# Reordering the opening of the first FFN and splitting the last row tile of a two-layer encoder step on one NeuronCore

## The chip, the core and the metric

The kernel runs on one NeuronCore of a Trainium2 chip. The five engines that matter here have queues of their own: TensorE (PE in the profile, with its weight loads as PEld), VectorE (DVE), ScalarE (ACT), GpSimd (POOL) and SyncE (SP, which only issues DMAs here). The metric is the device time of one execution in microseconds; the figure quoted is the median of several runs. A profile shows one further execution, and its span runs from the first to the last instruction of the program.

## The reference

Two layers are computed over 640 tokens of width 1024: 512 prompt tokens and 8 running streams of 16 tokens. Each layer is

```python
xp = xp + 0.5 * _swiglu(_rmsnorm(xp, norm_ffn1[l]), w_ffn1_gu[l], w_ffn1_down[l])
mp, ... = _mixer(_rmsnorm(xp, norm_mix[l]), ...)     # convolution branch and attention branch
xp = xp + mp
xp = xp + 0.5 * _swiglu(_rmsnorm(xp, norm_ffn2[l]), w_ffn2_gu[l], w_ffn2_down[l])
...
y_prompt = _rmsnorm(xp, norm_final)
```

with `_swiglu(h) = (silu(h @ w_g) * (h @ w_u)) @ w_down`, an inner width of 2816, and an RMS norm that divides a token by the root of the mean of its squares and multiplies by a gain. The same is done to the sample tokens. Everything is fp32.

## The kernel before

**Products in three passes.** The activations live in SBUF as eight tiles `x[0..7]`, 128 features by 640 tokens. Each fp32 operand is split into a high part, rounded to fp32r by ScalarE (`whi` for weights, `xhi` for activations), and a low part, the difference, made by VectorE (`wlo`, `xlo`). A product is the sum of three matmuls: high by high, and the two mixed ones. Thus no weight slab can be used before ScalarE has made its `whi` (L369) and VectorE its `wlo` (L375). A slab is 128x1024; `prep` (L355) makes `whi` and puts the `wlo` on a list, `flush` (L373) issues the list, `source` and `ahead` (L304, L397) make the sums of raw weights that some slabs need, and `slab(True)` (L380) takes the next slab and calls `prep` two slabs ahead without the flush.

**Seven products in place of eight.** Most groups multiply 2 by 2 blocks in a scheme with seven block products, in the order X11, X21, XN6, XT5, XT7, X22, XT4. One block product is 12 matmuls of 320 columns. The sums that such a scheme needs, of inputs, of weights and of outputs, are VectorE's work for the most part.

**The opening** (`opening`, L755) is the first FFN's start. Nine dummy matmuls run while the first loads arrive. Then, for each k of 0 to 7, `Expand.plain(k)` (L656) splits x[k] times its gain, L774 and L775 split 256 columns of a weight slab, and after each odd k the four products of two k's go into the PSUM accumulators `first[0]` and `first[1]`. After that come the squares of x[0..7] on ScalarE (`square`), added up on VectorE (`add`, tile `ssuma`). After the squares of k = 4 and k = 5, `out(0)` and `out(1)` copy the two accumulators out of PSUM (L795, L803). There are two accumulators of that kind, so the next product, `ps[2]`, waits for `out(0)`. In the middle of `ps[2]` TensorE sums `ssuma` over the partitions (`npsa`), ScalarE takes the root (L742), VectorE the reciprocal, and `spread` makes `rhoa`, the factor of every token, by which all later outputs of the FFN are multiplied.

**The first down unit** (`down_rows`, L1159). In the first FFN the inner tiles 0 to 3 are made by `opening`, and 4 and on by `gate_up` (L895). Between tiles 5 and 6 stands the first unit of the down projection, for output rows 0 to 3 (`second` is false) of inner tiles 0 to 3 (`sent` is true). Its block products go through PSUM pairs `daa`, `dba`, `dca`; `take` (L1199) adds a pair into x on VectorE, `stage` copies one out on ScalarE, and `send` adds it into x by DMA. `tail` (L1181) runs what tile 5 left over: silu(g) times rho (L1032), the product with u (L1069), and the split of the result (L1076, L1124). `place("d1")` then runs three combining instructions of that pair (L1134, L1136). The block XT4 of this unit writes the pair `daa` that `take(a, 1, t2)` has read.

**The end** (`Final.all`, L2168). The last down projection and the final norm are done in two shapes. Tokens 0 to 255 stay in feature order (`product`, `take`, `out`). The other 384 tokens are turned: three row tiles i = 0, 1, 2 of 128 tokens, each in two PSUM banks `rows[i][0]` and `rows[i][1]` of 512 features. For each, `half(i, h)` does six matmuls, `square(i, h)` is a sum of squares on ScalarE, `part` and `inverse` make the factor, `ahead` multiplies by the gain on VectorE before the factor is known, `scaled` multiplies by gain and factor in one VectorE instruction, and `rest` multiplies what `ahead` made by the factor on ScalarE.

**What sets the order.** In the opening, in the first down unit and at the end the mode is `order(ORDERED)`: TensorE, VectorE and ScalarE each take their instructions in the program's order. From inner tile 6 of an FFN up to its last chunk only TensorE's order is fixed (L1304), and the scheduler places the others.

All semaphores are set by the framework in which the kernel is written.

Of the kernel before, what the change touches and what calls it, by code (L numbers as in the profile page):

```python
# [16 lines left out]
P = 128  # L17
HP = P // 2
D = 1024
# [176 lines left out]
def trunk(ctx: ExitStack, tc: tile.TileContext, xin, wst, small, pbias, samplebias, kcache, vcache, gfin,  # L196
# [387 lines left out]
    class Expand(Stats):  # L584
# [71 lines left out]
        def plain(self, m):  # L656

            kp, odd = divmod(m, 2)
            n = f"{self.name}_{kp}"
            g = sm[:, self.goff + m : self.goff + m + 1]  # L660

            def low(lo, src, hi):
                DVE.scalar_tensor_tensor(out=lo, in0=src, scalar=g, in1=hi.bitcast(F32),
                                         op0=ALU.mult, op1=ALU.subtract)

            if odd:
                hi, lo = (z[:, 3:5] for z in self.ops[kp])
                ACT.activation(hi, halves(x[m]), AF.Copy, scale=g)
                low(lo, halves(x[m]), hi)
                return tuple(tuple(z[:, a] for a in range(2)) for z in (hi, lo))  # L670
            hi, lo = (self.fp.tile([P, 7, HT], F32R, name=f"x{i}{n}", tag=f"x{i}{kp}") for i in ("hi", "lo"))
            self.ops.append((hi, lo))
            if kp % 2 == 0:
                self.side = [hp.tile([P, T], F32R, tag=f"h{i}", name=f"x2{i}{n}") for i in ("hi", "lo")]
            c = slice(kp % 2 * HT, (kp % 2 + 1) * HT)
            out = (hi[:, X11], self.side[0][:, c]), (lo[:, X11], self.side[1][:, c])
            for a, (h, l) in enumerate(zip(*out)):
                src = x[m][:, a * HT : (a + 1) * HT]
                ACT.activation(h, src, AF.Copy, scale=g)
                low(l, src, h)  # L680
            return out
# [73 lines left out]
    def opening(fp, name, goff, n, pairs, tails):  # L755

        ACT.copy(early, epst)
        ex = Expand(fp, name, goff)  # L760
        h = []
        for i in range(2):
            ready.append(tuple(wp.tile([P, CH], F32R, tag=f"w{t}", name=f"w{t}{i}", bufs=3) for t in ("hi", "lo")))

        idle, row = att("idle"), tmp("row")[:, :P]
        DVE.memset(row, 1.0)
        for i in range(WAKE):
            PE.matmul(idle[:, :P], ones.to_broadcast([P, P]), row, start=i == 0, stop=i == WAKE - 1)
        first = [acc(f"po{name}_{i}") for i in range(2)]
        for k in range(KT):  # L770
            h.append(ex.plain(k))
            c = slice(k // 2 * 2 * P, (k // 2 + 1) * 2 * P)
            raw, (whi, wlo) = raws[k % 2], ready[k % 2]
            ACT.copy(whi[:, c], raw[:, c])  # L774
            DVE.tensor_tensor(out=wlo[:, c], in0=raw[:, c], in1=whi[:, c].bitcast(F32), op=ALU.subtract)  # L775
            if k % 2:
                for p, w in zip(first, ready):
                    for kk in (k - 1, k):
                        multiply(p, [z[:, kk * P : (kk + 1) * P] for z in w], h[kk], kk == 0, kk == KT - 1)
        used[0] = 2  # L780

        mixed = [z for kp in range(NP) for z in [ex.mixed(kp)] * 2]
        made = {2: (0,), 3: (1, 2, 3), 4: (4,), 5: (5, 6), 6: (7,)}
        us, gs, ps = [], [], first

        def out(i):

            j, up = divmod(i, 2)
            if not up:
                gs.append(tmp(f"g{name}_{j}"))  # L790
                if j:
                    scaled(gs[j], ps[i], ex.rho)
                    ACT.activation(gs[j], gs[j], AF.Silu)
                else:
                    ACT.copy(halves(gs[j]), two(ps[i]))  # L795
                return
            u = tmp(f"u{name}_{j}") if j > 1 else fp.tile([P, T], F32, tag="cap", name=f"u{name}_{j}", bufs=6)
            us.append(u)
            if j:
                scaled(u, ps[i], ex.rho)  # L800
                DVE.tensor_tensor(out=u, in0=u, in1=gs[j], op=ALU.mult)
            else:
                ACT.copy(halves(u), two(ps[i]))  # L803

        def begun():
            ex.total(att(f"nps{name}"))
            ex.root()
            ex.diagonal()

        at = {2: {6: begun}, 3: {1: lambda: ex.spread([att(f"nbc{name}_{a}")[:, :HT] for a in range(2)])}}  # L810
        prep(2)
        flush()
        for k in range(KT):
            ex.square(k)
            ex.add()
            if k in (4, 5):
                out(k - 4)
        for i in range(2, 2 * n):
            ps.append(acc(f"po{name}_{i}"))
            product(ps[i], h, at.get(i, {}))  # L820
            if i > 2:
                out(i - 1)
            if i == 3:
                g, u = gs[0], us[0]
                DVE.tensor_tensor(out=g, in0=g, in1=ex.rho, op=ALU.mult)
                ACT.activation(g, g, AF.Silu)
                DVE.tensor_tensor(out=u, in0=u, in1=ex.rho, op=ALU.mult)
            flush()
            for m in made.get(i, ()):
                next(mixed[m])  # L830
            if i == 3:
# [12 lines left out]
        ahead()  # L844
        out(2 * n - 1)
        tails += [lambda: pairs[1].odd(us[3]), pairs[1].mixed, pairs[1].fourth]
        ex.rest = None
        return ex
# [310 lines left out]
    def down_rows(fp, n, ms, pairs, tails, later, sent):  # L1159
# [49 lines left out]
        behind.clear()  # L1209
        prep(used[0] + 1)  # L1210
        begin()
        if not second:
            tail()
        flush()
        place("d1")
        mul(b, s0, 1, X21, True)
        with soon():
            take(b, 0, t1)
# [11 lines left out]
        with soon():  # L1230
            take(a, 1, t2, -0.5)
        send(c5, 1, t2)
        flush()
        ahead()
        mul(c, s2, 1, X22, False)
# [923 lines left out]
    class Final:  # L2159


        def __init__(self):
            self.st = Stats("f")
            self.ssum = pool[0].tile([P, FEAT], F32, tag="ssum", name="fsum", bufs=1)
            self.acc = sp.tile([P, 2 * GROUPS], F32, tag="facc", name="facc", bufs=1)
            self.root = sp.tile([P, 3 * GROUPS], F32, tag="froot", name="froot", bufs=1)

        def all(self, ops):  # L2168
# [37 lines left out]
            for k in range(1, 4):  # L2206
                self.out(k, rr)
            self.half(1, 0, ops, ws)
            self.square(1, 0)
            self.part(1)  # L2210
            self.half(1, 1, ops, ws)
# [1 line left out]
            for k in range(4, KT):  # L2213
                self.out(k, rr)
            self.inverse(1)
            for h in range(2):
                self.scaled(1, h)
            self.half(2, 0, ops, ws)
            self.square(2, 0)
            self.ahead(2)  # L2220
            self.part(2)
            self.half(2, 1, ops, ws)
            self.square(2, 1)
            self.ahead(2, 1)
            self.inverse(2)
            self.last(2)

        def product(self, m, ops, ws):
# [19 lines left out]
                PE.matmul(self.rows[i][h][:, o * P : (o + 1) * P], x[m][:, c], ident, is_transpose=True,  # L2248
                          start=o == 0, stop=False, skip_group_check=True)

        def half(self, i, h, ops, ws):

            tokens = slice(FEAT + i * P, FEAT + (i + 1) * P)
            c = slice(h * D // 2, (h + 1) * D // 2)
            for k, ((xh, xl), (wh, wl)) in enumerate(zip(ops, ws)):
                for j, (z, w) in enumerate(((xh, wh), (xl, wh), (xh, wl))):
                    PE.matmul(self.rows[i][h], z[:, tokens], w[:, c], start=False,
                              stop=k == len(ops) - 1 and j == 2, skip_group_check=True)

        def column(self, i, o):  # L2260
            return self.root[:, 3 * i + o :][:, 0:1]

        def square(self, i, h):
            ACT.activation(tmp(f"sqr{i}{h}")[:, : D // 2], self.rows[i][h], AF.Square,
                           accum_out=self.acc[:, 2 * i + h :][:, 0:1])

        def part(self, i):
            DVE.tensor_scalar(out=self.column(i, 0), in0=self.acc[:, 2 * i :][:, 0:1], scalar1=1.0 / D,
                              scalar2=EPS, op0=ALU.mult, op1=ALU.add)

        def inverse(self, i):
            ACT.activation(self.column(i, 1), self.acc[:, 2 * i + 1 :][:, 0:1], AF.Sqrt,
                           bias=self.column(i, 0), scale=1.0 / D)
            DVE.reciprocal(self.column(i, 2), self.column(i, 1))

        def ahead(self, i, h=0):
            c = slice(h * D // 2, (h + 1) * D // 2)
            DVE.tensor_tensor(out=self.y[i][:, c], in0=self.rows[i][h], in1=self.g[:, c], op=ALU.mult)

        def last(self, i):  # L2280
            for o, w, engine in ((0, 3, DVE), (3, 2, ACT), (5, 3, DVE)):
# [198 lines left out]
```

## Time and profile before

| | |
|---|---|
| time, median of 3 runs | 2467.57 us (2467.53 to 2467.99) |
| time of the profiled execution | 2468.21 us |
| its span | 2466.4 us |
| PE busy | 2458.3 us (100%) |
| DVE busy | 2196.8 us (89%) |
| ACT busy | 1396.9 us (57%) |
| POOL busy | 329.7 us (13%) |
| HBM over the span | 101 GB/s |
| granted TensorE clock | 1.000 |

A row of a timeline gives start and length in us, the engine, the source line, the operation, the output and inputs by their names in the program, the shape, and in brackets how long the engine sat idle before it and what ended that. "xN" means that N such instructions were merged into one row, and the length is then that of the whole group. A row of a view of waits gives the engine and line that waited, what released it, the total in us, the number of waits and the longest. An "engine" with a q at its end is the engine's queue, which issues DMAs.

### The profile page before, as it was taken

How to read it: one execution, taken by the hardware profiler on the slowest of the kernel's cores; microseconds unless marked ns; L12 is line 12 of the kernel's file. 1: busy time of each engine (PE TensorE's matmuls, PEld its weight loads, DVE VectorE, ACT ScalarE, POOL GpSimd, SP SyncE). 2: the span in 40 equal slices, each digit the busy share in tenths (PEclk: the TensorE clock that was granted, in tenths of full speed). 3: DMA queues.
4: the chain of work that ended last, by engine and by line, in shares of the span. 5: the costliest groups of instructions: out<-in, count | busy, mean ns of one | idle time of the engine just before them, and what ended most of it. 6: DMA issues, size and time to landing. Idle time of an engine off the chain costs nothing.

```text
span 2466.4 us, 44136 instructions
## 1 busy us (share of the span) xinstructions
PE 2458.3 (100%) x17234; PEld 2409.1 (98%) x17234; DVE 2196.8 (89%) x3725; ACT 1396.9 (57%) x2246; POOL 329.7 (13%) x495
## 2 busy tenths in 40 slices
PE   9999999999999999999999999999999999999999
PEld 9999999889999999999999999998899999999998
DVE  7999999888998899998799999988889979999997
ACT  6555556665655555555665555566656556555555
POOL 0211112211110001011001111121110000111111
PEclk9999999999999999999999999999999999999999
DMA  4553444335443334445334343453454433444444
GB/s 156 138 126 100 121 118 122 111 112 175 116 130 123 87 102 112 108 118 123 107 97 109 109 119 101 118 129 102 139 160 122 122 115 94 108 113 107 113 118 118
DMA packets 115282, 290.93 MB, mean 118 GB/s; under 512 B 13216, under 2 KB 53664, under 8 KB 115072
## 3 DMA queue, kind: packets, MB, share of 16 engines
q1 hardware_dynamic: 69840, 220.10, 28.3%
q0 software_dynamic: 44800, 67.75, 14.6%
q8 instruction: 135, 2.21, 0.4%
q14 instruction: 75, 0.61, 0.1%
q10 hardware_dynamic: 432, 0.25, 0.0%
HBM read 241.57 MB, written 7.94 MB: 101 GB/s over the span
## 4 chain that ended last, share of the span: by engine, by line
PE 97%; DMA 1%; DVE 1%; ACT 0%; issue 0%; SPq 0%; DVEq 0%; ACTq 0%
PE pab L469 13%; PE paa L469 11%; PE pcb L469 6%; PE pca L469 6%; PE daa L1175 6%; PE dab L1175 5%; PE po L445 5%; PE qa L469 4%; PE pbb L469 3%; PE pba L469 3%; PE dca L1175 3%; PE dcb L1175 3%; PE ma_qk L469 2%; PE ma_cv L469 2%; PE pv L1872 2%; PE qc L469 2%
## 5 line engine op out<-in xcount | busy, mean ns | idle before, releaser
L369 ACT CAST whi<-raw 128x1024 fp32r<-128x1024 f32 (+1 forms) x564 | 500.1, 892 | 376.1 <-DVE raw L298 63.6
L375 DVE TENSOR_TENSOR wlo<-raw,whi 128x1024 fp32r<-128x1024 f32 (+1 forms) x602 | 580.0, 967 | 135.4 <-ACT whi L369 131.8
L369 ACT CAST whi<-s 128x1024 fp32r<-128x1024 f32 (+1 forms) x166 | 155.2, 935 | 287.3 <-issue 111.3
L469 PE MATMUL pab<-xhib,whi 128*128 128x320 f32 x704 | 217.5, 309 | 0.0
L469 PE MATMUL pab<-xhib,wlo 128*128 128x320 f32 x704 | 217.0, 308 | 0.0
L469 PE MATMUL pab<-xlob,whi 128*128 128x320 f32 x704 | 217.0, 308 | 0.0
L469 PE MATMUL paa<-xhia,whi 128*128 128x320 f32 x640 | 197.7, 309 | 0.0
L469 PE MATMUL paa<-xloa,whi 128*128 128x320 f32 x640 | 197.5, 309 | 0.0
L469 PE MATMUL paa<-xhia,wlo 128*128 128x320 f32 x640 | 197.4, 308 | 0.0
L375 DVE TENSOR_TENSOR wlo<-s,whi 128x1024 fp32r<-128x1024 f32 (+1 forms) x169 | 179.1, 1060 | 3.6 <-ACT whi L369 3.6
L1197 POOL DMA_DIRECT2D x<-c_a x80 | 70.0, 1014 | 568.3 <-ACT ahia L1076 244.8
L1197 POOL DMA_DIRECT2D x<-c_b x72 | 63.1, 1009 | 582.2 <-ACT ahib L1076 205.8
L469 PEld LDWEIGHTS pab<-xhib,whi 128*128 128x128 f32 x704 | 132.1, 188 | 0.9 <-issue 0.9
L469 PEld LDWEIGHTS pab<-xlob,whi 128*128 128x128 f32 x704 | 132.2, 188 | 0.0
L469 PEld LDWEIGHTS pab<-xhib,wlo 128*128 128x128 f32 x704 | 132.1, 188 | 0.0
L469 PEld LDWEIGHTS paa<-xhia,whi 128*128 128x128 f32 x640 | 120.1, 188 | 0.6 <-issue 0.4
L469 PEld LDWEIGHTS paa<-xloa,whi 128*128 128x128 f32 x640 | 120.2, 188 | 0.2 <-DVE xloa L712 0.2
L469 PEld LDWEIGHTS paa<-xhia,wlo 128*128 128x128 f32 x640 | 120.1, 188 | 0.0
L298 DVE TENSOR_TENSOR raw<-s,raw 128x512 f32<-128x512 f32 x166 | 113.1, 682 | 0.0
L469 PE MATMUL pcb<-xhib,wlo 128*128 128x320 f32 x352 | 108.7, 309 | 0.0
L469 PE MATMUL pcb<-xlob,whi 128*128 128x320 f32 x352 | 108.5, 308 | 0.0
L469 PE MATMUL pcb<-xhib,whi 128*128 128x320 f32 x352 | 108.5, 308 | 0.0
(896 smaller groups left out, 8248.3 us busy)
## 6 DMA issues: line engine op xcount, KB each, us to landing
raw<-in_wst SPq DMA_DIRECT2D x374, 512.0 KB, 3.7
x<-c_a POOLq DMA_DIRECT2D x80, 160.0 KB, 4.4
x<-c_b POOLq DMA_DIRECT2D x72, 160.0 KB, 3.5
one<-in_wst POOLq DMA_DIRECT2D x40, 256.0 KB, 3.5
lent<-in_wst POOLq DMA_DIRECT2D x36, 256.0 KB, 3.8
kc<-in_kcache SPq DMA_DIRECT2D x32, 256.0 KB, 5.0
vc<-in_vcache SPq DMA_DIRECT2D x16, 512.0 KB, 4.6
x<-u_a POOLq DMA_DIRECT2D x40, 160.0 KB, 4.3
```

The lines of the kernel that those rows point to most:

```text
L298: DVE.tensor_tensor(out=out, in0=a, in1=b, op=op)
L369: ACT.copy(hi[:, d], src[:, c])
L375: DVE.tensor_tensor(out=lo, in0=src, in1=hi.bitcast(F32), op=ALU.subtract)
L445: PE.matmul(ps[:, a, :HT], w, x[a] if isinstance(x, tuple) else x[:, a * HT : (a + 1) * HT], start=first and j == 0 and not seeded, stop=l ...
L469: PE.matmul(ps, a, b, start=start and kp == 0 and j == 0, stop=stop and kp == NP - 1 and j == 2, skip_group_check=True)
L1175: PE.matmul(ps[u], w, y, start=start and i == 0 and j == 0, stop=i == 1 and j == 2, skip_group_check=True)
L1197: POOL.dma_start(x[ms[2 * u + r]][:, cols], z[:, u], accum_op=ALU.add)
L1872: PE.matmul(pv[t], xx[:, t * P : (t + 1) * P], w[:, kk * AW : (kk + 1) * AW], start=c == 0 and kk == 0 and j == 0, stop=c == KT // 2 - 1 a ...
```

## The change

Five edits in the first FFN and the end:

1. The odd tile x[1] is split in two column halves, ScalarE's cast and VectorE's difference in turn (`plain`).
2. The high part of the very first weight piece (k = 0) is made by VectorE, ahead of all else, in place of ScalarE.
3. `out(0)` and `out(1)` stand after the squares of k = 2 and 3 in place of 4 and 5.
4. In the first down unit `tail()` and `place("d1")` are put off until `take(a, 1, t2)` and its `send`.
5. At the end: row tile 1 gets `ahead(1)` between its first half and its squares, and then only its second half is scaled by VectorE; `rest(1)` scales the first on ScalarE, which issues its DMA too. The last half of row tile 2 is done in two quarters of 256 columns of the same bank, each with its matmuls, squares and product with the gain; the sum of squares gets one more column, and a second `part` adds the first quarter's.

```diff
@@ plain
             if odd:
                 hi, lo = (z[:, 3:5] for z in self.ops[kp])
-                ACT.activation(hi, halves(x[m]), AF.Copy, scale=g)
-                low(lo, halves(x[m]), hi)
+                for c in (slice(0, 1), slice(1, 2)) if m == 1 else (slice(0, 2),):
+                    ACT.activation(hi[:, c], halves(x[m])[:, c], AF.Copy, scale=g)
+                    low(lo[:, c], halves(x[m])[:, c], hi[:, c])
@@ opening
         first = [acc(f"po{name}_{i}") for i in range(2)]
+        c = slice(0, 2 * P)
+        DVE.tensor_copy(ready[0][0][:, c], raws[0][:, c])
         for k in range(KT):
...
-            ACT.copy(whi[:, c], raw[:, c])
+            if k:
+                ACT.copy(whi[:, c], raw[:, c])
...
             ex.square(k)
             ex.add()
-            if k in (4, 5):
-                out(k - 4)
+            if k in (2, 3):
+                out(k - 2)
@@ down_rows
         begin()
-        if not second:
+        put_off = sent and not second
+        if not second and not put_off:
             tail()
         flush()
-        place("d1")
+        if not put_off:
+            place("d1")
         mul(b, s0, 1, X21, True)
...
         send(c5, 1, t2)
+        if put_off:
+            tail()
+            place("d1")
         flush()
         ahead()
@@ Final
-            self.acc = sp.tile([P, 2 * GROUPS], F32, tag="facc", name="facc", bufs=1)
+            self.acc = sp.tile([P, 2 * GROUPS + 1], F32, tag="facc", name="facc", bufs=1)
...
             self.half(1, 0, ops, ws)
+            self.ahead(1)
             self.square(1, 0)
             self.part(1)
             self.half(1, 1, ops, ws)
...
             self.inverse(1)
-            for h in range(2):
-                self.scaled(1, h)
+            self.scaled(1, 1)
+            self.rest(1)
             self.half(2, 0, ops, ws)
             self.square(2, 0)
             self.ahead(2)
             self.part(2)
-            self.half(2, 1, ops, ws)
-            self.square(2, 1)
-            self.ahead(2, 1)
-            self.inverse(2)
+            for e in range(2):
+                self.half(2, 1, ops, ws, e)
+                self.square(2, 1, e)
+                self.ahead(2, 1, e)
+                if e == 0:
+                    self.part(2, 1)
+            self.inverse(2, 2)
             self.last(2)
...
+        def piece(e):
+            return slice(0, D // 2) if e is None else slice(e * D // 4, (e + 1) * D // 4)
...
+        def part(self, i, h=0):
+            z = self.column(i, 0)
+            if h:
+                DVE.scalar_tensor_tensor(out=z, in0=self.acc[:, 2 * i + h :][:, 0:1], scalar=1.0 / D, in1=z,
+                                         op0=ALU.mult, op1=ALU.add)
...
```

`half`, `square` and `ahead` get an argument e that cuts their columns with `piece`; `inverse` gets the column of the sum of squares that it takes.

More of the change, by code (lines that the diff above doesn't have):

```diff
@@ L2249, in turned, with half @@
                           start=o == 0, stop=False, skip_group_check=True)
-        def half(self, i, h, ops, ws):
+        @staticmethod
+        def piece(e):
+            return slice(0, D // 2) if e is None else slice(e * D // 4, (e + 1) * D // 4)
+        def half(self, i, h, ops, ws, e=None):
             tokens = slice(FEAT + i * P, FEAT + (i + 1) * P)
-            c = slice(h * D // 2, (h + 1) * D // 2)
+            o = self.piece(e)
+            c = slice(h * D // 2 + o.start, h * D // 2 + o.stop)
             for k, ((xh, xl), (wh, wl)) in enumerate(zip(ops, ws)):
                 for j, (z, w) in enumerate(((xh, wh), (xl, wh), (xh, wl))):
-                    PE.matmul(self.rows[i][h], z[:, tokens], w[:, c], start=False,
+                    PE.matmul(self.rows[i][h][:, o], z[:, tokens], w[:, c], start=False,
                               stop=k == len(ops) - 1 and j == 2, skip_group_check=True)
@@ L2261, in column, with square, inverse, ahead @@
             return self.root[:, 3 * i + o :][:, 0:1]
[L2263 to L2272, printed above, removed]
+        def square(self, i, h, e=None):
+            o = self.piece(e)
+            ACT.activation(tmp(f"sqr{i}{h}{e}")[:, o], self.rows[i][h][:, o], AF.Square,
+                           accum_out=self.acc[:, 2 * i + h + (e or 0) :][:, 0:1])
+        def part(self, i, h=0):
[3 more added lines that the diff above has]
+                                         op0=ALU.mult, op1=ALU.add)
+            else:
+                DVE.tensor_scalar(out=z, in0=self.acc[:, 2 * i :][:, 0:1], scalar1=1.0 / D,
+                                  scalar2=EPS, op0=ALU.mult, op1=ALU.add)
+        def inverse(self, i, h=1):
+            ACT.activation(self.column(i, 1), self.acc[:, 2 * i + h :][:, 0:1], AF.Sqrt,
                            bias=self.column(i, 0), scale=1.0 / D)
             DVE.reciprocal(self.column(i, 2), self.column(i, 1))
-        def ahead(self, i, h=0):
-            c = slice(h * D // 2, (h + 1) * D // 2)
-            DVE.tensor_tensor(out=self.y[i][:, c], in0=self.rows[i][h], in1=self.g[:, c], op=ALU.mult)
+        def ahead(self, i, h=0, e=None):
+            o = self.piece(e)
+            c = slice(h * D // 2 + o.start, h * D // 2 + o.stop)
+            DVE.tensor_tensor(out=self.y[i][:, c], in0=self.rows[i][h][:, o], in1=self.g[:, c], op=ALU.mult)
         def last(self, i):
```

## The prediction

> **What bounds the kernel now.** The page's first part and the chain of work that ended last are read first, then who waited for whom on PE in the first 300 us.
>
> ```profile
> PE 2458.3 (100%) x17234; PEld 2409.1 (98%) x17234; DVE 2196.8 (89%) x3725; ACT 1396.9 (57%) x2246; POOL 329.7 (13%) x495
> PE 97%; DMA 1%; DVE 1%; ACT 0%; issue 0%; SPq 0%; DVEq 0%; ACTq 0%
> PE poa L445 <- ACT ga L795: 0.7, 1, 0.7
> PE poa L445 <- ACT whi L774: 0.3, 1, 0.3
> PE poa L445 <- DVE xloa L663: 0.3, 1, 0.3
> PEld daa L1175 <- DVE x L1202: 0.4, 1, 0.4
> ```
>
> PE is the path for 97% of the span. The change removes no matmul: it can gain only where PE stands still, which is 0.7 + 0.3 + 0.3 us in the opening, 0.4 us in the first down unit, and what runs behind the last matmul. Against that, VectorE is busy for 89% and for longer stretches without a gap, so I ask at each edit what VectorE finishes next.
>
> **The opening (edits 1 to 3).** Rows of PE's chain, of ScalarE and VectorE, and VectorE's waits from 31 to 102 us:
>
> ```profile
> 20.47 0.67 ACT L795 COPY ga<-poa 128x640 f32<-128x640 f32 x1
> 18.71 6.41 DVE L298 TENSOR_TENSOR ssuma<-ssuma,sqa 128x640 f32<-128x640 f32 x7
> 26.74 0.44 PE npsa L552 x39
> 25.53 1.28 ACT L742 ACT_TABLE_LOAD   x1
> 27.27 0.27 ACT L742 ACTIVATE nrmsa<-npsa,epst 128x5 f32<-128x5 f32 x1 [0.46 <-PE npsa L552]
> DVE ga L582 <- ACT rhoa L579: 2.1, 1, 2.1
> DVE xloa L712 <- ACT xhia L706: 1.3, 2, 0.7
> DVE eloa L1124 <- ACT ehia L1093: 0.5, 1, 0.5
> DVE ga L1032 <- ACT ga L1019: 0.4, 1, 0.4
> DVE wlo L375 <- ACT whi L369: 0.4, 1, 0.4
> 80.00 1.22 DVE L375 TENSOR_TENSOR wlo<-s,whi 128x1024 fp32r<-128x1024 f32 x1 [0.39 <-ACT whi L369]
> 81.28 0.19 PEld L469 LDWEIGHTS paa<-xhia,wlo 128*128 128x128 f32 x1
> ```
>
> Edit 3 starts `ga` two squares earlier, each about as long as this copy of the same shape (0.67), so it ends near 19.9 in place of 21.14 and the stall of 0.7 goes. Edits 1 and 2 shorten the first stalls by some 0.2 of 0.6: VectorE's differences of x[0] and x[1] remain in a row on one engine. PE would reach `npsa` some 1.0 us earlier, near 25.7, and the sum `ssuma` is complete then (18.71 + 6.41 = 25.12, and 0.25 later because two squares now stand behind the copies). But the root behind it waits for a table load that ScalarE's own row of work holds until 25.53 + 1.28 = 26.81. So the root starts at 26.83, not 27.27: 0.44 earlier. Everything from `rhoa` on moves by that 0.44. From there VectorE waits for ScalarE alone, and those ScalarE instructions wait for VectorE in turn; PE stands behind none of them before the last but one, at 93.23. At 81.22 it delivers the `wlo` that PE loads at 81.28, 0.06 later: no slack. PE therefore arrives there at most 0.44 earlier, whatever it gained before. **Term: -0.44** (bounds: -1.0 if PE doesn't need that `wlo` so soon, 0 if `ssuma` or the copy on VectorE is late).
>
> **The first down unit (edit 4).** VectorE from 93 to 106 us, the unit's first block on PE, and PE's weight load in tile 6's block XN6:
>
> ```profile
> 93.23 0.82 DVE L1032 TENSOR_TENSOR ga<-ga,rhoa 128x640 f32<-128x640 f32 x1 [0.42 <-ACT ga L1019]
> 94.83 0.68 DVE L375 TENSOR_TENSOR wlo<-lent,whi 128x512 fp32r<-128x512 f32 x1
> 96.64 0.81 DVE L1124 TENSOR_TENSOR aloa<-doa,ahia 128x640 fp32r<-128x640 f32 x1
> 97.37 0.48 DVE L1134 SCALAR_TENSOR_TENSOR doa<-dea,doa 128x320 f32<-128x320 f32 x1
> 97.78 0.81 DVE L1124 TENSOR_TENSOR aloa<-dea,ahia 128x640 fp32r<-128x640 f32 x1
> 99.31 0.88 DVE L1202 SCALAR_TENSOR_TENSOR x<-dba,x 128x320 f32<-128x320 f32 x2
> 100.11 0.88 DVE L1202 SCALAR_TENSOR_TENSOR x<-daa,x 128x320 f32<-128x320 f32 x2
> 104.83 1.22 DVE L375 TENSOR_TENSOR wlo<-s,whi 128x1024 fp32r<-128x1024 f32 x1
> 90.07 1.76 PE daa L1175 x12
> 106.29 0.19 PEld L469 LDWEIGHTS paa<-xhia,wlo 128*128 128x128 f32 x1
> ```
>
> Block by block at 1.76 us, XT7 ends at 90.07 + 5 x 1.76 = 98.87. The `take` of it ran only at 100.11 to 100.99, because `tail` and `d1` stood in front: that is PE's wait of 0.4 before XT4. Moved behind the `take`, they no longer hold it: it starts at 99.03, and PE gains 0.39.
>
> Now what is queued behind the moved work on VectorE. In the program's order that is the `wlo` of tile 6's first slab, the weight sums `s`, the `take` of `dca`, one more sum, and the `wlo<-s` at 104.83, which tile 6 needs for its block XN6 at 106.29. From the start of `take` to the end of `wlo<-s` before: 106.05 - 100.11 = 5.94. The moved work, by starts: `ga` and product 94.83 - 93.23 = 1.60, the difference 97.37 - 96.64 = 0.73, three combinations at 97.78 - 97.37 = 0.41: 3.56 together, and 0.1 for dependences no longer covered. VectorE would idle while it waits for XT7, and `wlo<-s` would end at 99.03 + 5.94 + 3.66 = 108.6. PE, 0.39 early, wants it at 105.90 and gets it at 108.67: a new stall of 2.8, or 108.67 - 106.29 = 2.4 later than before; I take 0.1 off for starts that overlap. The blocks behind it move along with PE, as VectorE does, so I count the delay once. The DMAs of `send` that wait for these takes leave POOL's queue earlier by that edit, and PE reads none of those columns of x in this stage: nothing. **Term: +2.3** (bounds: -0.39 if the scheduler puts `s` first, +2.8 if the gain before XT4 doesn't come).
>
> **The end (edit 5).** VectorE and ScalarE around row tile 1, row tile 2's end, and two rows that show tiles shared by engines:
>
> ```profile
> 2442.75 5.92 PE pdf L2232 x48
> 2455.40 5.48 PE prow L2257 x24
> 2453.40 0.60 ACT L2264 ACTIVATE sqr<-prow 128x512 f32<-128x512 f32 x1 [2.05 <-DVE yrow L2278]
> DVE ss L2067 <- ACT ss L2066: 2.0, 1, 2.0
> 2457.55 0.15 DVE L2268 TENSOR_SCALAR froot<-facc 128x1 f32<-128x1 f32 x1
> 2457.62 1.66 DVE L2307 SCALAR_TENSOR_TENSOR x<-x,sm,frr 128x256 f32<-128x256 f32 x4
> 2459.23 0.16 DVE L2274 RECIPROCAL froot<-froot 128x1 f32<-128x1 f32 x1
> 2455.69 0.72 ACT L2302 ACTIVATE yrow<-yrow,froot 128x512 f32<-128x512 f32 x1 [0.43 <-DVE froot L2274]
> 2460.91 0.70 ACT sqr L2264 x2
> 2462.96 0.35 ACTq L2287 DMA_DIRECT2D out_yrows<-yrow  x1
> 2461.62 0.69 DVE yrow L2278
> 2462.42 0.42 DVE yrow L2286
> ```
>
> Two engines that read one PSUM tile go one behind the other: the squares of row tile 0 waited 2.05 for VectorE's `ahead`, and L2067 waits for L2066 though they read other columns. With that, in the program's order (last digits of the time, 2400 left off):
>
> - `ahead(1)` takes the place of `part` (57.55) on VectorE, to 58.22; `square(1, 0)`, which `part` had already awaited there, now runs 58.30 to 58.98, and VectorE stands 0.8 us until `part` at 59.02.
> - Four `out` follow, 59.09 on, 1.61 from first to `inverse`: the reciprocal is at 60.70 (59.23 before), so `scaled(1, 1)` and `rest(1)` start at 60.91.
> - `rest(1)` takes ScalarE until 61.63, its DMA issue of 0.35 until 62.02. Queued behind both is `square(2, 0)`, whose matmuls end at 2455.40 + 3 x 5.48 / 4, so 59.51, and which runs 62.03 to 62.71. SP has one issue fewer, and nothing waits there. Then `ahead(2)` to 63.42.
> - The first quarter's six matmuls, at 5.92 / 48 = 0.12, are done at 60.25; its squares end at 63.14, and its `ahead`, some 0.41 against 0.69 for twice the columns, at 63.82.
> - The second quarter's matmuls write the same bank and I let them wait for that: 63.88, six at 0.12 with 0.3 for start and drain: done at 64.89, against 2455.40 + 5.48 = 60.88 before.
> - Behind it come squares of 0.46 and an `ahead` of 0.41 in place of 0.70 and 0.69 (estimates from those two rows). The last scaling starts at 65.92, against 62.42. What follows (three DMAs, closing waits) is unchanged.
>
> **Term: +3.5.** No row shows PE writing one half of a bank while another engine reads the other half; the nearest are the two above, so I let it wait. If it doesn't, ScalarE's queue still holds: the second quarter's squares follow at 63.85 and the last scaling at 64.9, +2.5. The Trainium skill, "PSUM — Partial Sum Buffer", section "PSUM bank collisions raise a hardware error", speaks against the quarters: any two engines on one bank and quadrant collide, disjoint columns too, a TensorE write among them, so software must put them in turn. By it the sum is the one with +3.5; no run here shows the pair with TensorE.
>
> **Sum.** -0.44 + 2.3 + 3.5 = +5.4 us. On the profiled execution: span 2466.4 to 2471.8, time 2468.21 to 2473.6. The median of the runs is 0.64 under that execution: 2467.57 + 5.4 = **2472.9**. About 0.2%, 4.9 us, is what a measurement of this kernel can tell from no change; the forecast lies just beyond it.
>
> **Rivals.**
> - *PE doesn't wait for the readers of the other quarter*: end +2.5, time 2471.9. For it: no row shows the wait. Against: both shared-tile rows.
> - *The sums run ahead of `tail`*: no new stall, -0.39 in that term: 2467.57 - 0.44 - 0.39 + 3.5 = 2470.2. For it: at 97.78 an instruction of tile 6 (`aloa<-dea`) stood inside `d1`. Against: the `take` of `dba`, whose matmuls end at 90.07 + 2 x 1.76 = 93.59, ran at 99.31, in program order.
> - *VectorE and ScalarE take what is ready, at both places* (the other side): then the sums go first, and `square(2, 0)` stays in front of `rest(1)`. The end still pays the turn about the bank, some 0.8 (squares 0.46 and `ahead` 0.41 between the quarters): 2467.57 - 0.44 - 0.39 + 0.8 = 2467.5, not slower. It decides where `s<-raw` starts before the moved `ga` and `sqr` of row 2 before `rest`. Against it: the same `take`.
> - *The whole 1.0 of the opening reaches the end*: 2472.3. Against: 0.06 between 81.22 and 81.28.
> - *The last quarter at a lower clock.* PE would stand from 60.25 to 63.88, 3.6 us, five times its longest wait before (0.7). If the six matmuls and their drain (0.9) then took twice as long: 2473.8. The granted clock is 1.000 over the whole span and no row has such a gap, so the trace can't decide it. The Trainium skill, "TensorE: Matmul & The Clock Gate", section "What's actually happening", gives the rule: about 3.4 us idle closes the gate, in free-running windows; no run here shows it.
>
> **How the numbers follow.** Forecast 0.50, PE not waiting 0.12, sums first 0.12, clock 0.10, readiness 0.08, whole opening 0.08. The range 2469.5 to 2474.2 takes in all but readiness and the edges of the others. Slower by over 0.2% (above 2472.5): some 0.32 of the forecast's 0.50, the clock's 0.10 and 0.03 of the whole opening, 0.45. Faster by that much would need 4.9 us, more than all stalls named: 0.02. Within 0.2%: 0.53.
>
> **What would show it.** Right: `nrmsa` near 26.83; the wait of `daa` for x gone; a PE wait of 2 to 3 us on `paa` for `wlo` near 106; PE idle for over 3 us inside `prow`, released by VectorE's `yrow`; `sqr` of row 2 behind ScalarE's DMA issue. Wrong: no PE wait near 106 (second rival), or both quarters' matmuls without a gap (first).

## The result, and the profile after

| | before | after |
|---|---|---|
| time, median of 6 runs each, taken together | 2467.65 us (2467.13 to 2467.99) | 2476.25 us (2475.3 to 2476.99) |
| ratio after to before, 95% interval | | 1.0033 [1.0023, 1.0043] |
| span of the profiled execution | 2466.4 us | 2474.6 us |
| mean granted TensorE clock | 1.000 | 0.998 |

The change makes the kernel slower by 8.6 us. The forecast was 2472.9 with a range up to 2474.2: the sign is right, the size is not.

The first part of the page of after, and its row of the granted clock:

```profile
PE 2461.8 (99%) x17240; PEld 2412.4 (97%) x17240; DVE 2197.7 (89%) x3729; ACT 1398.0 (56%) x2249; POOL 329.4 (13%) x495
...
PEclk9999999999999999999999999999999999999999
```

The page hardly tells the two kernels apart. PE has six more matmuls, and yet 3.5 us more of busy time (2461.8 against 2458.3): matmuls that last longer are the first hint. The clock row can't show it, since a slice is a fortieth of the span, 62 us, and 9 stands for anything from 0.9 up. The waits of PE in after say more:

```profile
PE prow L2275 <- DVE yrow L2303: 3.6, 1, 3.6
PE paa L469 <- ACT c_a L989: 2.9, 1, 2.9
```

The short waits on `poa` and on x are gone (1.7 us in all before), and two long ones stand in their place, both where the prediction put them. (A third, of 1.1 us ahead of the dummy matmuls, is in every run, before's too.)

**The first down unit.** PE's timeline of after around the first of them (start, length, engine, line, operation):

```profile
105.41 0.31 PE L469 MATMUL pba<-xhia,wlo 128*128 128x320 f32 x1
108.61 0.41 PE L469 MATMUL paa<-xhia,whi 128*128 128x320 f32 x1 [2.89 <-ACT c_a L989]
...
109.78 0.47 PE L469 MATMUL paa<-xhia,whi 128*128 128x320 f32 x1
...
112.98 0.38 PE L469 MATMUL pca<-xhia,whi 128*128 128x320 f32 x1
113.20 0.31 PE L469 MATMUL pca<-xloa,whi 128*128 128x320 f32 x1
...
113.94 0.31 PE L469 MATMUL paa<-xhia,whi 128*128 128x320 f32 x1
```

The same matmuls in PE's timeline of before:

```profile
105.99 0.31 PE L469 MATMUL pba<-xhia,wlo 128*128 128x320 f32 x1
106.14 0.31 PE L469 MATMUL paa<-xhia,whi 128*128 128x320 f32 x1
...
109.66 0.31 PE L469 MATMUL paa<-xhia,whi 128*128 128x320 f32 x1
```

PE is 0.58 early in front of the stand (105.41 for 105.99) and 2.47 late behind it (108.61 for 106.14). The stand isn't the end of it: the 24 matmuls from there to 113.94 take 5.33 us, where before they took 3.52. Thirteen of them, from 109.78 to 113.20, follow one another at 0.27 us in place of 0.15. Two windows of after, the second right behind those matmuls (length, then busy time and number of instructions on PE, PEld, DVE, ACT and POOL, the granted clock, DMA share, GB/s):

```profile
108.60:113.00 4.40, 4.39 (x19) 4.24 (x20) 4.00 (x7) 1.94 (x4) 2.75 (x4) 0.63 1.02 170
113.20:118.00 4.80, 4.80 (x34) 4.80 (x34) 2.93 (x5) 1.82 (x3) 0.00 (x0) 1.00 0.76 246
```

The clock was granted at 0.63 on average over the first and at 1.00 over the second, with PE busy throughout both; over the slow stretch alone, 109.78 to 113.20, it is 0.51. So the stage costs 4.28 at 113.94 (against 109.66), of which 5.33 - 3.52 = 1.81 comes after the stand: 1.5 in the thirteen slow matmuls, and 0.3 in the first six, which run at a granted clock of 0.97 and of which the third had to wait for its weights.

Who held PE up: VectorE's and ScalarE's timelines of after.

```profile
98.79 0.89 DVE L1206 SCALAR_TENSOR_TENSOR x<-daa,x 128x320 f32<-128x320 f32 x2 [2.54 <-PE daa L1179]
99.60 0.81 DVE L1036 TENSOR_TENSOR ga<-ga,rhoa 128x640 f32<-128x640 f32 x1
...
103.53 0.82 DVE L1128 TENSOR_TENSOR aloa<-dea,ahia 128x640 fp32r<-128x640 f32 x1
...
105.79 0.69 DVE L298 TENSOR_TENSOR s<-s,raw 128x512 f32<-128x512 f32 x1
...
107.79 1.22 DVE L375 TENSOR_TENSOR wlo<-s,whi 128x1024 fp32r<-128x1024 f32 x1
```

```profile
106.59 1.04 ACT L369 CAST whi<-s 128x1024 fp32r<-128x1024 f32 x1 [3.93 <-DVE s L298]
107.54 0.70 ACT L1193 ACTIVATE t_a<-daa 128x640 f32<-128x640 f32 x1
108.14 0.42 ACT L989 COPY c_a<-paa 128x320 f32<-128x320 f32 x1
```

The moved work (99.60 on) stands ahead of the weight sums `s` on VectorE. ScalarE's row has nothing to do for 3.93 us, since its next instruction casts those sums; the two behind it need nothing of them, but wait in its order. The last, `c_a`, empties the PSUM pair that the block XN6 writes, and ends at 108.56: PE starts at 108.61. The third matmul needs the `wlo` that VectorE ends at 109.01, and its weights are loaded at 109.06.

**The end.** Timelines of after: ScalarE, VectorE and PE from row tile 2 on, and row tile 0's `rest` as a reference.

```profile
2459.87 0.72 ACT L2327 ACTIVATE yrow<-yrow,froot 128x512 f32<-128x512 f32 x1 [0.43 <-DVE froot L2298]
...
2465.00 0.72 ACT L2327 ACTIVATE yrow<-yrow,froot 128x512 f32<-128x512 f32 x1 [0.97 <-DVE froot L2298]
2465.75 0.38 ACTq L2328 DMA_DIRECT2D out_yrows<-yrow  x1
2466.17 0.60 ACT L2283 ACTIVATE sqr20None<-prow 128x512 f32<-128x512 f32 x1 [0.45 <-ACT yrow L2327]
```

```profile
2467.56 0.42 DVE L2303 TENSOR_TENSOR yrow<-prow,gfin 128x256 f32<-128x256 f32 x1
...
2470.54 0.75 DVE L2311 TENSOR_SCALAR yrow<-yrow,froot 128x384 f32<-128x384 f32 x2
```

```profile
2464.12 0.28 PE L2275 MATMUL prow<-wlo,ahib 128*128 128x256 f32 x1
2468.03 0.39 PE L2275 MATMUL prow<-whi,ahib 128*128 128x256 f32 x1 [3.63 <-DVE yrow L2303]
...
2469.05 0.41 PE L2275 MATMUL prow<-wlo,ahib 128*128 128x256 f32 x1
```

Row tile 1's `rest` and its DMA issue hold up row tile 2's squares on ScalarE; the first quarter's product with the gain ends on VectorE at 2467.98, and only then does PE write the second quarter. From `rest` of row tile 0 to the last scaling it is 2470.54 - 2459.87 = 10.67 us, against 2462.42 - 2455.69 = 6.73 before: +3.94. The start of that reference row is 2459.87 - 2455.69 = 4.18 late, so opening and down unit together made 4.18, the end 3.94: 8.1 of the span's 8.2.

### The profile page after: what moved, and what is told of

Same layout as the page of the kernel before. It is cut to its first block, busy times and chain, and to the rows that moved or that the text cites. A ratio compares the mean times of both kernels' runs of the same rounds, so it can differ in the third digit from the quotient of the medians.

```text
span 2474.6 us, 44154 instructions
## 1 busy us (share of the span) xinstructions
PE 2461.8 (99%) x17240; PEld 2412.4 (97%) x17240; DVE 2197.7 (89%) x3729; ACT 1398.0 (56%) x2249; POOL 329.4 (13%) x495
## 4 chain that ended last, share of the span: by engine, by line
PE 99%; DVE 1%; ACT 0%; issue 0%; ACTq 0%; DVEq 0%; POOL 0%; POOLq 0%
PE pab L469 13%; PE paa L469 11%; PE pcb L469 6%; PE pca L469 6%; PE daa L1179 6%; PE dab L1179 5%; PE po L445 5%; PE qa L469 4%; PE pbb L469 3%; PE pba L469 3%; PE dca L1179 3%; PE dcb L1179 3%; PE poa L445 2%; PE ma_cv L469 2%; PE ma_qk L469 2%; PE pv L1881 2%
## 5 line engine op out<-in xcount | busy, mean ns | idle before, releaser
L469 PE MATMUL pcb<-xhib,whi 128*128 128x320 f32 x352 | 108.6, 308 | 0.0
L469 PE MATMUL pcb<-xlob,whi 128*128 128x320 f32 x352 | 108.6, 308 | 0.0
```

The source lines that it names most:

```text
L469: PE.matmul(ps, a, b, start=start and kp == 0 and j == 0, stop=stop and kp == NP - 1 and j == 2, skip_group_check=True)
```

## The experiments

All comparisons are of 11 runs against 33 of the kernel before on the same chip, whose median was 2467.76, 2467.63 and 2467.86 us in the three groups. The theory at their outset: three places add up, the opening for nothing, the down unit by its stall and a clock that falls behind it, the end by a queue and a bank. The rival: the parts act on each other, or the time beyond the forecast has another source.

**One part alone.** Each of these three takes over the named edits of the change as they stand and nothing else.

Edits 1 to 3 (`open_only`):

> Edits 1 to 3 alone. Theory (the opening's gain is lost again on VectorE's ring before 81 us): PE about 0.7 us early near 20 us, some 0.2 us early at 81 us, time 0.2 us under the kernel before (2467.4). Rival (the opening's gain is passed on whole): 0.7 us or more under (2466.9).

Edit 4 (`tail_only`):

> Edit 4 alone. Theory (VectorE's moved work delays wlo<-s, PE stands about 3 us before XN6 and then runs at a lower clock for 3 to 4 us): 0.4 gained before XT4, 3.0 lost in the stall, 1.8 lost to the clock, time 4.4 above the kernel before (2472.0). Rival (the three edits hinder each other and this one alone is harmless): within 0.5 of the kernel before.

Edit 5 (`end_only`):

> Edit 5 alone. Theory (the end's chain is its own): last scaling 3.9 us later against PE's last whole half, time 3.9 above the kernel before (2471.6). Rival (the end is longer only because PE comes late from the first FFN): within 0.5 of the kernel before.

| kernel | median us | less the before | ratio, 95% interval |
|---|---|---|---|
| open_only | 2468.13 | +0.37 | 1.0002 [0.9993, 1.0011] |
| tail_only | 2472.41 | +4.65 | 1.0018 [1.0009, 1.0027] |
| end_only | 2471.77 | +4.01 | 1.0017 [1.0008, 1.0026] |

The sum, +9.0, is the whole change's +8.6 within the intervals: the parts add up. No gain of the opening can be seen in the time; the down unit costs twice its term.

Two stretches inside the traces tell the parts apart more finely than the times do. From the root of the opening (`nrmsa` on ScalarE) to the first matmul of XN6 in tile 6 it is 78.87 us in before and 81.51 in after and in `tail_only`; to the block 24 matmuls on it is 82.39, and 86.84 in both others: +4.45. From `rest` of row tile 0 to the last scaling it is 6.73 in before, 10.67 in after and 10.22 in `end_only`: +3.94 and +3.49.

**Is it the clock?** `tail_twice` is `tail_only` with the block X21 of tile 6, just ahead of the stand, computed a second time to the same values: 12 more matmuls, 1.76 us of PE's time.

```diff
             mul(pb, s0, 1, X21, every, True, True)
+            if n == "a0_6":
+                mul(pb, s0, 1, X21, every, True, True)
```

> Edit 4 alone, and tile 6's block X21 is done twice (12 matmuls more, the second pass starts its sums anew and gives the same result). Theory (the standing of PE for 3 us lowers the clock): PE stands for 1.3 us in place of 3.1, the granted clock stays at 1.00 behind it, and the time is 1.6 under edit 4 alone (2470.4) although 1.76 us of matmuls are added. Rival (the low clock comes by chance of a window or from the memory traffic): no change against edit 4 alone, clock 0.6 for 3 us again. Second rival (PE doesn't wait for VectorE there): 1.8 slower than edit 4 alone.

Measured 2470.67 us, +2.91, ratio 1.0013 [1.0004, 1.0022]: 1.74 under `tail_only` of the same group, with more work. The waits of PE in `tail_only`, then in `tail_twice`:

```profile
PE paa L469 <- ACT c_a L985: 2.9, 1, 2.9
```

```profile
PE paa L469 <- ACT c_a L985: 1.1, 1, 1.1
```

And the window from 108 to 114 us, in the columns of above, in `tail_only`, in `tail_twice`:

```profile
108.00:114.00 6.00, 4.72 (x21) 4.56 (x22) 5.27 (x8) 3.22 (x7) 4.02 (x5) 0.74 0.82 137
```

```profile
108.00:114.00 6.00, 4.87 (x33) 4.45 (x32) 5.59 (x9) 4.10 (x8) 4.10 (x5) 1.00 0.76 119
```

With the stand cut to 1.1 us the clock holds at 1.00, and the window shows 33 matmuls where it showed 21. The two intervals overlap, so the 1.74 isn't settled by the ratios alone. Inside the traces it is 1.54: from XN6's first matmul on, the 24 take 5.33 us in `tail_only`, as in after, and 3.79 in `tail_twice`. (XN6 itself starts 81.51 behind the root in `tail_twice` as in the other two.) So the clock, not some other effect of edit 4, is 1.54 of the 1.81 that came on top of the stand; the other 0.27, over the 3.52 of before, is the slow start, which stays. These are one trace of each; over the eleven runs of each the mean clock agrees, if coarsely: 0.999 of full in ten runs of `tail_only`, 1.000 in eight of `tail_twice`.

**Is it what the moved work stands in front of?** `tail_late` is edit 4 with `tail()` and `place("d1")` moved further, behind the unit's last `flush`, and so behind the sums `s`.

```diff
-        if put_off:
-            tail()
-            place("d1")
         flush()
         ahead()
...
             take(a, 1, t1, -0.5)
         flush()
+        if put_off:
+            tail()
+            place("d1")
```

> Edit 4 with the tail and d1 put off further, behind the unit's last flush, so that the weight sums and wlo<-s come first on VectorE. Theory (what counts is what the moved work stands in front of): no wait of PE before XN6, the 0.4 before XT4 stays gained, 0.4 under the kernel before (2467.2). Rival (any delay of the tail costs, since VectorE is full): a stall of over 1 us somewhere before 130 us, time above the kernel before.

Measured 2467.35 us, -0.28, ratio 0.9999 [0.999, 1.0008]. The waits of PE in `tail_late`:

```profile
PE idle L768 <- POOL epst L484: 1.1, 1, 1.1
PE poa L445 <- DVE xloa L663: 0.4, 1, 0.4
PE poa L445 <- ACT whi L774: 0.2, 1, 0.2
```

Neither the wait on `daa` nor that on `paa` is left. All of edit 4's 4.65 is the order of the moved work against `s`. The 0.4 that the edit was to gain can't be told from nothing in the time, but the trace has it: XN6 starts 78.45 us behind the root, for 78.87 in before.

**What the end is made of.** `row1_only` has the first half of edit 5 (row tile 1), `quarters_only` the second (the quarters in one bank, row tile 1 as before), and `quarters_bank` the quarters with the second one in a PSUM bank of its own. `end_bank` is the whole of edit 5 with that bank.

```diff
+            self.ahead(1)
             self.square(1, 0)
...
-            for h in range(2):
-                self.scaled(1, h)
+            self.scaled(1, 1)
+            self.rest(1)
```

```diff
-            self.rows.append([att(f"prow2{h}") for h in range(2)])
+            self.rows.append([att(f"prow2{h}") for h in range(3)])
...
+        def bank(self, i, h, e):
+            return self.rows[i][2][:, : D // 4] if e == 1 else self.rows[i][h][:, self.piece(e)]
```

> Of edit 5 only row tile 1 (ahead(1) before its squares, rest(1) on ScalarE); the last half stays whole. Theory (ScalarE's row: square(2, 0) behind rest(1) and its DMA issue): last scaling some 1.9 us later, time 1.9 above the kernel before (2469.5). Rival (the quarters are the whole cost): within 0.4 of the kernel before.

> Of edit 5 only the quarters, in one bank. Theory (the second quarter's matmuls wait for both readers of the first): PE stands about 1.6 us between the quarters, the clock stays, time 1.4 above the kernel before (2469.0). Rival (the quarters cost nothing while VectorE is the bound there): within 0.4 of the kernel before.

> The quarters alone, the second one in a PSUM bank of its own. Theory (the wait is one for the bank): PE doesn't stand between the quarters, and the last scaling is where it was before, bound by VectorE: within 0.3 of the kernel before (2467.7). Rival (the second quarter waits for the first's readers whatever bank it writes): as the quarters in one bank, 1.4 above the kernel before.

> The whole of edit 5, with the second quarter's matmuls in a PSUM bank of their own. Theory (one bank makes TensorE wait for the first quarter's readers, row tile 1's part adds its queue on ScalarE): no wait of TensorE on prow for VectorE, so no drop of the clock there either; row tile 1's +1.9 stays and the quarters add 0.6, so some +2.5 over the kernel before, 2470.2, or 1.6 under edit 5 as it is (2471.8). Rival (the cost of edit 5 is all ScalarE's queue, whatever the bank): 2471.8 as with one bank.

| kernel | median us | less the before | ratio, 95% interval | end, in the trace |
|---|---|---|---|---|
| row1_only | 2469.52 | +1.89 | 1.0008 [0.9999, 1.0017] | +1.76 |
| quarters_only | 2469.11 | +1.48 | 1.0005 [0.9996, 1.0013] | +1.52 |
| quarters_bank | 2468.22 | +0.59 | 1.0002 [0.9993, 1.0011] | +0.09 |
| end_bank | 2469.80 | +1.94 | 1.0008 [1.0, 1.0017] | +2.08 |

The last column is the stretch from `rest` of row tile 0 to the last scaling, less the 6.73 of before. `quarters_bank` was expected within 0.3 of before: the trace says so, the time is too coarse to.

The two halves make 3.4 in time, and the whole edit alone made 4.0; in the traces they make 3.28, against 3.49 in `end_only` and 3.94 in after. What parts those last two is the clock. PE's timeline of `quarters_only` first:

```profile
2461.17 0.39 PE L2265 MATMUL prow<-whi,ahib 128*128 128x256 f32 x1 [1.66 <-DVE yrow L2293]
...
2461.86 0.28 PE L2265 MATMUL prow<-wlo,ahib 128*128 128x256 f32 x1
```

Here the stand is 1.66 us, and the six matmuls end at 2462.14, 0.97 after the first began. In after, with row tile 1's queue in front, the stand is 3.63, and they take 2469.46 - 2468.03 = 1.43: 0.46 more. The window of after around them:

```profile
2468.00:2469.50 1.50, 1.43 (x6) 1.14 (x6) 0.04 (x1) 0.00 (x1) 0.00 (x0) 0.61 0.00 0
```

The clock stood at 0.61. `end_only` has the same stand (3.64 us), and a window there shows the same six matmuls, the only ones in it:

```profile
2463.00:2466.00 3.00, 0.98 (x6) 0.78 (x6) 1.45 (x7) 1.28 (x4) 0.00 (x0) 0.76 0.11 39
```

They take 0.98, as in `quarters_only`: here the low clock begins at 2464.54, just behind the last of them (2464.39). So the same stand cost the matmuls behind it 0.46 in one execution and nothing in the other. With a bank of its own the second quarter doesn't wait at all; in PE's timeline of `end_bank` it follows the first:

```profile
2459.22 0.28 PE L2271 MATMUL prow<-wlo,ahib 128*128 128x256 f32 x1
2459.34 0.28 PE L2271 MATMUL prow<-whi,ahib 128*128 128x256 f32 x1
```

`end_bank` came to +1.94, where +2.5 was expected and the rival had +4.0. In the traces the wait for the bank is 3.49 - 2.08 = 1.41 of the end's cost, and the clock 0.45 more where it falls in time; the rest is row tile 1's queue on ScalarE (1.76 alone), beside which quarters in banks of their own add 0.3.

**The opening, and versions without the losses.** `open12_only` has edits 1 and 2 alone; `best3` has edit 3 and the late tail, `best` edits 1 to 3 and the late tail, both with the end as before.

> Edits 1 and 2 alone: x[1] in column halves and the first high part on VectorE; the copies out(0) and out(1) stay behind the squares of k = 4 and 5. All three opening edits together came 0.4 above the kernel before, where 0.2 under was expected. If these two cost what edit 3 gains (the copy ua on ScalarE or the extra instructions hold up the stage): +0.3 to +0.6 over the kernel before. If all three simply don't reach the end: within 0.2 of it, with npsa's root at the same place as before (near 27.27).

> Edit 3 alone, and tail and d1 put off behind the unit's last flush, so behind the weight sums that tile 6 needs; the end as before. Theory: the 0.4 before XT4 is gained without the stall behind it, and the root starts 0.2 to 0.4 earlier: 0.3 to 0.7 under the kernel before, 2467.1. Rival (nothing gained before the last products reaches the end): 2467.6, the same as before.

> Edits 1 to 3 with tail and d1 behind the unit's last flush; the end as before. Theory: the sum of the two measured apart (+0.37 and -0.28): 2467.7 +- 0.5. If edits 1 and 2 are the cause of the opening's loss, this stands 0.3 to 0.6 over the kernel with edit 3 alone of the same batch; if not, the two agree within 0.2.

| kernel | median us | less the before | ratio, 95% interval |
|---|---|---|---|
| open12_only | 2468.06 | +0.20 | 1.0 [0.9991, 1.0009] |
| best3 | 2467.71 | -0.15 | 1.0 [0.9991, 1.0008] |
| best | 2467.51 | -0.35 | 0.9998 [0.9989, 1.0007] |

All three are the kernel before, as far as these runs can tell, and neither the 0.3 to 0.7 expected of `best3` nor the 0.2 of `open_only` shows; `best` has edits 1 and 2 and isn't above `best3`, so no loss of theirs shows either. Both stand some 9 us under the whole change, and none beats the kernel before beyond its interval. In time, what the parts of the opening are worth stays open below 2 us or so, the half width of these intervals.

Whether edit 3 brings its 0.44 can't be told. ScalarE's timeline of after from `ga` to the root, and then the end of that of `open_only`:

```profile
19.25 0.67 ACT L799 COPY ga<-poa 128x640 f32<-128x640 f32 x1
19.82 0.74 ACT L732 ACTIVATE sqa<-x 128x640 f32<-128x640 f32 x1
20.68 0.69 ACT L807 COPY ua<-poa 128x640 f32<-128x640 f32 x1
...
25.80 1.28 ACT L743 ACT_TABLE_LOAD   x1
27.10 0.27 ACT L743 ACTIVATE nrmsa<-npsa,epst 128x5 f32<-128x5 f32 x1
```

```profile
25.53 1.28 ACT L743 ACT_TABLE_LOAD   x1
26.83 0.27 ACT L743 ACTIVATE nrmsa<-npsa,epst 128x5 f32<-128x5 f32 x1
```

In both the root stands right behind the table load, where in before it came 0.46 later, with PE's `npsa`. `open_only` has it at 26.83, the predicted place; after has it at 27.10, and `best` and `best3` at 27.36 and 27.37, no earlier than before (27.27). In after `ua` is asked for before PE has done with its accumulator, a gap of 0.12 (20.56 to 20.68); in `best` it waited 0.43 for PE. But the place of the root isn't steady: the nine traces with the opening of before have it anywhere from 26.59 (`tail_late`) to 28.09 (`tail_twice`). In that scatter neither the hit of `open_only` nor the miss of after says what edit 3 is worth. What is steady is the way from the root on: to the `wlo<-s` that before starts at 80.00 it is 52.73 us in before, and within 0.01 of that in all fourteen traces.

## Why the prediction was right and wrong

The sum failed by 2.8 us in the trace (+8.1 for +5.4), term by term:

| term | predicted | trace of after | alone, in its trace | alone, in time |
|---|---|---|---|---|
| opening | -0.44 | -0.2 | -0.44 | +0.37 |
| first down unit | +2.3 | +4.4 | +4.45 | +4.65 |
| end | +3.5 | +3.94 | +3.49 | +4.01 |

The opening's -0.2 and -0.44 are the place of the root, 27.10 and 26.83 for 27.27, and both lie within its scatter. The unit's +4.4 is 4.18 + 0.2.

- **The mis-sized term is the first down unit**, in the step "a new stall of 2.8, or ... 2.4 later than before", which ended with the stall. The stall itself was nearly right: the load of XN6's `wlo` was predicted at 108.67 and came at 109.06. What failed is that a stand of almost 3 us was priced as idle time alone. Behind it the clock fell to 0.51, and the same 24 matmuls took 1.81 us longer; `tail_twice`, with the stand filled, shows the clock held and 1.54 of that gone. The prediction had this mechanism among its rivals, but only for the last quarter, with the argument that PE stands there five times as long as ever before (as ever between products: ahead of the dummy matmuls it had waited 1.1). The stand of 2.8 that it had just worked out for the down unit was four times as long by the same measure, and wasn't asked the same question.
- Of the 2.15 that the term lacks (+4.45 for +2.3), the clock is 1.54; the other 0.6 is the stall. `aloa<-dea` was left out of the moved work because it stood as tile 6's own; it stayed in VectorE's row (103.53 to the next start at 104.27, 0.74), and `wlo<-s` ended at 109.01, not 108.6, in an execution that began the unit 0.2 early. And PE's first matmul of XN6 was let go not by that `wlo` but by ScalarE's `c_a`, behind `whi<-s` in ScalarE's order. The prediction asked what is queued behind the moved work on VectorE, and not what ScalarE has queued behind the cast of its result.
- **The opening** is left open. Its mechanism is in the traces: with edit 3 the root stands right behind the table load, and its shift reaches the `wlo` at 80.00 whole. Its size isn't shown: in after the table load slid from 25.53 to 25.80, in `open_only` it stood at 25.53, and 0.44 is less than a third of the scatter of 1.5 us. The time (+0.37, with an interval from -1.7 to +2.7 us) excludes neither the term nor either of its bounds.
- **The end** held step by step. From `rest` of row tile 0 to the second quarter's first matmul 63.88 - 55.69 = 8.19 us were predicted, and 2468.03 - 2459.87 = 8.16 came. From there to the last scaling 65.92 - 63.88 = 2.04 were predicted and 2.51 came: the quarter's six matmuls at the lower clock. In `end_only`, where they ran at the full clock, the whole way is 10.22, for 10.23 predicted. That PE waits for the readers of the other quarter, for which no row of before spoke directly, is shown by `quarters_only` (1.66 of wait) against `quarters_bank` and `end_bank` (none). The wait is a semaphore of the framework, which orders instructions by the tile: whether the chip would have needed it isn't shown. By the Trainium skill, "PSUM — Partial Sum Buffer", section "PSUM bank collisions raise a hardware error", it would, and software has to set it; no run here tries the two without it.
- The rival of PE not waiting gave +2.5 for the end; built as `end_bank`, which makes its condition true, it measured +1.94 in time and +2.08 in the trace. The rivals of readiness and of sums first fall with VectorE's order at 98.79 to 107.79: everything ran in the program's order.
- The range ended at 2474.2 because the clock was counted once. With the lower clock at both stands, and the 1.54 and 0.45 that the traces show for it, the predicted sum would have been 5.4 + 2.0 = 7.4 us, 2475.0.

## What to carry to other kernels

Moving work away from in front of one wait puts it in front of all that follows on its engine, so walk that engine's order on to the next result that the bound engine needs, and then the order of the engine that turns this result into something else: here 3.6 us of work moved to save 0.4, and cost 4.65 in front of the sums but nothing behind them. Price a new stand of TensorE of about 3 us as the stand and a stretch at a lower clock behind it: here 1.5 us more in the middle of the program, and 0.45 or nothing where only six short matmuls followed. In this framework a tile split for the sake of overlap must be split in its banks too, or the second part waits for the readers of the first.

## What the runs showed of the hardware

The granted clock fell after stands of 2.89 us (after, down unit), 2.88 (`tail_only`) and 3.63 us (after, end), and not after 1.13 (`tail_twice`). The 1.66 us of `quarters_only` decide nothing: the six matmuls behind it follow at full rate (0.12 apart but for the first), but they end 0.97 us behind the restart, and soon after the clock is down, with PE idle again:

```profile
2463.00:2466.00 3.00, 0.00 (x0) 0.00 (x0) 0.93 (x4) 0.51 (x1) 0.00 (x0) 0.59 0.48 175
```

It didn't fall at once. In after the low stretch ran from 109.78, 1.17 us behind the restart, to 113.20: 3.42 us. In `tail_only` the same stand ended at 109.28, and PE's timeline shows the low stretch from about 111.0 to 114.3, 1.7 us behind the restart and as long:

```profile
110.87 0.43 PE L469 MATMUL paa<-xhia,whi 128*128 128x320 f32 x1
111.11 0.47 PE L469 MATMUL paa<-xloa,whi 128*128 128x320 f32 x1
...
114.04 0.44 PE L469 MATMUL pca<-xhia,whi 128*128 128x320 f32 x1
114.31 0.32 PE L469 MATMUL pca<-xloa,whi 128*128 128x320 f32 x1
```

At the end of the program, where PE stops for good, the clock fell in every trace too, but not after one fixed time: in the eleven traces without a stand in the last half it was from 2.3 us behind the last matmul (`open_only`, 2460.80 to 2463.1) to 5.3 (before, 2460.87 to 2466.2).

The Trainium skill, "TensorE: Matmul & The Clock Gate", section "What's actually happening", has the clock halved after an idle window of about 3.4 us, restored after a busy one, and the windows free-running. The length of the low stretch agrees with it (3.42 us), and so does a start that differs against the restart from one execution to the next. The stand that brings it on does not: 2.89 and 2.88 us were enough here, and 2.3 at the end of `open_only`, so a stand somewhat below that window has to be counted too. How much shorter it may be isn't settled between 1.13 and 2.3 us.

The start of the program may vary in the same way. One product of the opening, in PE's timeline of after and then of before:

```profile
5.86 0.47 PE L445 MATMUL poa<-xloa,whi 128*128 128x320 f32 x1
```

```profile
6.03 0.31 PE L445 MATMUL poa<-xloa,whi 128*128 128x320 f32 x1
```

The same shape lasted 0.47 in one execution and 0.31 in the other, the lengths that the low and the full clock gave above. That one execution differs from the next by the clock of its first microseconds is an argument from those lengths, not a test, and the profile doesn't bear it out: its granted clock is 1.00 from 5.0 to 7.5 us in both. Were it so, it would be a reason why the place of the root scatters, and why the opening's fractions of a microsecond can't be told in the time.
